# P^T by VectorE's 32x32 transposes and a trip through DRAM in a two-layer attention encoder

## The chip, the cores and the metric

The kernel runs on one core of one Trainium2 chip. The metric is the device time of one execution in microseconds, of which the median over the runs is given. Smaller is better. A core has a matrix engine (TensorE, called PE here; its weight loads are listed apart as PEld), VectorE (DVE), ScalarE (ACT), GpSimd (POOL), a queue engine (SyncE, SP) from which this kernel starts nearly all its DMA transfers, and 16 DMA engines which carry these out. TensorE takes operands from the on-chip SBUF and writes into PSUM; VectorE and ScalarE read both; DMA connects SBUF and DRAM.

## The reference

512 tokens of width 1024 pass two layers, each of them: RMS norm, one input projection (q, k, v of 16 heads of width 64, and a gate), attention, times silu(gate), an output projection, and the residual. Layer A has three groups of heads with dilated windows, merged by their softmax denominators; layer B attends to a neighbourhood on an 8 x 64 grid.

```python
def reference(x, ...):
    for i in range(DEPTH):                       # 2
        hn = rms_norm(x, norm_gain[i])
        y = mixer_a(...) if i % N_MIXERS == 0 else mixer_b(...)
        x = x + y.astype(x.dtype)

# mixer_a, of each group g (window, dilation) in ((128, 1), (512, 4), (2048, 16))
logits = jnp.einsum('brhqd,brhkd->brhqk', qb, kb) * scale + bias
p = jnp.exp(jnp.where(valid, logits, NEG_INF) - mx)
out = jnp.einsum('brhqk,brhkd->brhqd', p, vb) / denom[..., None]
# merged by softmax over the groups of log(denom) + mx; y * silu(gate) @ w_out

# mixer_b
logits = jnp.einsum('bhcqd,bhrcjd->bhcqrj', qr, kr) + bias
p = jax.nn.softmax(where(col_valid, logits, NEG_INF), axis=-1)
out = jnp.einsum('bhcqrj,bhrcjd->bhcqd', p, vr)
```

In both layers P (queries on partitions, keys along the row) has to be turned before it is multiplied with v, since TensorE sums over partitions and the keys must lie there.

## The kernel before

All is float32. A projection is made of triples (`mm3`, L211): operands are split into a high and a low part, and three matmuls of parts add up in PSUM. The weights come from DRAM in pieces of 1024 columns (`raws`, L165: `wraw`, three buffers, issued on SP), are split by ACT (`wh`, L126) and by DVE or POOL (`wl`, L130), with four buffers each, and are used by `project` and `project_t` (L230, L246) and `out_product` (L755). Heads are worked on in pairs, `hc` = 0 to 7 in each layer; "heads 0 to 13" are the pairs 0 to 6.

PE's order of work is written out by hand. `main` (L935) yields after every triple of the projections; `side` (L948) is everything else, above all the attention. `run` (L722) joins them: every matmul adds its modelled ns to `clock` (a triple of 512 columns adds 3 x 213 = 640, a triple of 384 columns 480, a 128x128 transpose 109), and whenever `clock` has reached the due time, the side work goes on to its next `yield`. `yield 2500` means: go on 2,500 modelled ns later; `yield "wait", key, 12000` means: 12,000 after the moment at which `stamp[key]` was set. So the numbers in the yields are distances in PE's order. PE executes strictly in that order. The other engines' orders, the DMA queue of SP among them, are laid down by a scheduler when the kernel is built; each engine then works through its own list and waits at semaphores.

Layer A, one pair (`attn_a`, L604): two halves `u`. In each, `scores(u)` (L610) multiplies q and k of two query tiles and two heads into four PSUM banks, `softmax` (L645) adds the bias `e0`, `e12` and takes the minimum on DVE (signs are turned round, L652, L663), the exponent on ACT (L674) and the scaling on ACT (`normalise`, L541, L542); the result is `pr`, four buffers of 128x512. Then for each of the four `pr`, `turn_p` (L678) makes four 128x128 transposes on PE into a PSUM bank and DVE copies it into `pts` (L682). After the second half `weigh` (L684) multiplies `pts` with v into one bank `o`, and `put_y` (L544) multiplies by the gate (L565) and splits the result into `y_h`, `y_l`. A pair's time in layer A is 69.9 us, in layer B 29.2 us.

Layer B (`side_b`, L830): transposes of q and k, `scores(0)`, `scores(1)` (two banks each), `turn_p` four times (four, four, three and three transposes; DVE's copy is L904), then `weigh` (L906) and `put_y`. `raw` (L396, tag `rawk`, two buffers) holds q, k, v of the pair; its v is read by `weigh`.

`bias_a` (L573) and `bias_b` (L589) load the bias tables of a pair with six DMAs on SP, from lines in DRAM which overlap from partition to partition. There are two buffers, so the loads for pair hc + 2 can start when pair hc has read its own. `residual` (L787) loads x in pieces into tiles of the tag `pt`, which is also that of `pts`.

Of the kernel before, what the change touches and what calls it, by code (L numbers as in the profile page):

```python
# [12 lines left out]
F32 = mybir.dt.float32  # L13
# [8 lines left out]
P = 128  # L22
S = 512
D = 1024
DH = 64
NHC = 8
KT = 8
# [14 lines left out]
def tile_hybrid_encoder(  # L42
# [13 lines left out]
    nc = tc.nc  # L56
# [242 lines left out]
    def tjr(t):  # L299
        return t.rearrange("p (t j r) -> p t j r", t=4, j=4)  # L300
# [93 lines left out]
    st = {}  # L394
# [194 lines left out]
    def bias_b(hc):  # L589
# [11 lines left out]
                )  # L601
        return e

    def attn_a(hc):  # L604
        e0, e12 = st.pop(("e", hc))
        q0h, q0l, q12, k0h, k0l = st.pop(("q", hc))
        k12, v12 = st.pop(("k12", hc))
        pts = {}
# [36 lines left out]
        def softmax(hd, t, lg, cs, n):  # L645
            pr = wk.tile([P, 512], F32, tag="p", name="p", bufs=4)
            mn = wk.tile([P, 4], F32, tag="mn", name="mn", bufs=4)
            if t == 0:
                nc.gpsimd.memset(pr[:, 0:64], 0.0)
            if t == 3:  # L650
                nc.gpsimd.memset(pr[:, 192:256], BIG)
            nc.vector.tensor_tensor_reduce(  # L652
                out=pr[:, cs : cs + n],
                in0=lg[:, cs : cs + n],
                in1=e0[:, hd, cs : cs + n],
                scale=1.0,
                scalar=3.0e38,
                op0=ALU.add,
                op1=ALU.min,
                accum_out=mn[:, 0:1],  # L660
            )
# [12 lines left out]
            nc.scalar.activation(row, row, AF.Exp, bias=mn[:, 1:2], scale=-1.0, accum_out=mn[:, 2:3])  # L674
            normalise(row, mn)
            return pr

        def turn_p(hd, t, pr):  # L678
            tp = bank("tp")
            for i in range(4):  # L680
                transpose(tp[:, i * P : (i + 1) * P], pr[:, i * P : (i + 1) * P])
            nc.vector.tensor_copy(pts[hd][:, t, :], tp)  # L682

        def weigh():  # L684
            o = bank("o")
            mms = []
            for g in range(2):
                for j in range(4):
                    c = 256 + P * g
                    mms.append((  # L690
                        lambda t_, j=j: tjr(t_)[:, :, j, :],
                        lambda hs, j=j, c=c: v12[:, j, c + hs.start : c + hs.stop],
                        lambda hd, c=c + 32 * j: pts[hd][:, :, c : c + 32],
                    ))
            for i in range(4):
                f, d, n = (512 * i - 384, P * i - P, P) if i else (0, 0, 384)
                mms.append((
                    lambda t_, d=d, n=n: sb(t_, d, [[n, 2], [1, P]]),
                    lambda hs, i=i: v0[hc % 2][:, i, hs],
                    lambda hd, f=f, n=384 if i else 1664: sb(pts[hd], f, [[n, 2], [1, P]]),  # L700
                ))
            side_by_side(o, mms)
            return o

        for u in range(2):
            yield 2500 if hc < NHC - 1 else 1200
            held = scores(u)
            yield 5500 if hc < NHC - 1 else 3200
            for args in held:
                turn_p(*args)  # L710
                yield 1700 if hc < NHC - 1 else None
        if hc == NHC - 1:
            yield from v_a(hc)
            stamp["ya", "turned"] = 0
        o = weigh()
        if hc == NHC - 2:
            gap[0] = cycle((500, 500, 700))
            yield "wait", ("gate", hc), 1500
        put_y(hc, o, True, hc == NHC - 1)
        yield  # L720
# [64 lines left out]
            yield from step(k, (7,))  # L785

    def residual(src):  # L787
        st["xr"] = []
        for f in range(0, KT, 2):
            if f % 4 == 0:  # L790
                xs = wk.tile([P, 4, S], F32, tag="pt", name="xr")
            nc.sync.dma_start(xs[:, f % 4 : f % 4 + 2, :], src[:, f : f + 2, :])
            st["xr"] += [xs[:, f % 4, :], xs[:, f % 4 + 1, :]]
            yield 1000

    def sink_a(f, acc):
# [19 lines left out]
    def main_b(hc):  # L816
# [10 lines left out]
        nc.scalar.activation(eg, gt, AF.Tanh, scale=0.5)  # L827
        gated(hc, gt, eg)

    def side_b(hc):  # L830
# [17 lines left out]
        put_k([(kh, kl, tp)], 3)  # L848
        stamp["qk", hc] = 0
        yield 1750  # L850
        pts = {}

        def scores(u):
            if u == 0:
                for hd in range(2):
                    pts[hd] = wk.tile([P, 4, 512], F32, tag="pt", name="pt").rearrange("p a c -> p (a c)")
            lgs = [bank("log") for _ in range(2)]
            for b in (2 * u, 2 * u + 1):
                if b < 3:
# [38 lines left out]

        def turn_p(hd, u, pr):
            tp = bank("tp")  # L900
            n = 512 if u == 0 else 384
            for i in range(n // P):
                transpose(tp[:, i * P : (i + 1) * P], pr[:, i * P : (i + 1) * P])
            nc.vector.tensor_copy(pts[hd][:, 512 * u : 512 * u + n], tp[:, :n])  # L904

        def weigh():  # L906
            o = bank("o")
            mms = []

            for d, n, m, f in (  # L910
                (64, 128, 0, 0), (0, 64, 0, 768), (192, 256, 2, 384), (448, 64, 3, 832),
                (64, 256, 1, 128), (320, 128, 3, 640),
            ):
                mms.append((
                    lambda t_, d=d, n=n: t_[:, d : d + n],
                    lambda hs, m=m: raw[:, m, 256 + hs.start : 256 + hs.stop],
                    lambda hd, f=f, n=n: pts[hd][:, f : f + n],
                ))
# [10 lines left out]
        if hc == NHC - 1:  # L929
            stamp["yb", "turned"] = 0  # L930
        o = weigh()
        put_y(hc, o, False, hc == NHC - 1)
        yield

    def main():  # L935
# [148 lines left out]
```

## Time and profile before

| | |
|---|---|
| median of 3 runs | 904.92 us (903.37 to 907.12) |
| the profiled execution, its own time | 908.62 us |
| its span, first to last instruction | 906.7 us |
| mean granted TensorE clock | 0.994 |
| DMA | 88.31 MB, mean 97 GB/s; SP's queue 29.3% of the 16 engines' span |
| tp<-ident,p: transposes of P on PE | 368 |
| L682 DVE copy pt<-tp 128x512 | 64 of 689 ns |
| L904 DVE copy pt<-tp 128x512, 128x384 | 16 of 691 ns, 16 of 558 ns |
| PE matmul o<-pt,rawk 128x128 (runs of 32), o<-pt,raw 128x128 (whole rows) | 276 ns, 285 ns |
| wraw<-in_w | 95 of 512 KB, 38 of 384 KB, 10 smaller |
| e<-l_d, eb<-lb_d, eb<-gb_d | 32 of 112 KB and 16 of 128 KB; 16 of 128 KB; 32 of 32 KB |

Matmuls overlap one another: the 272 ns that the profile gives for one transpose are its own length from start to modelled end, not its step on PE. What a piece of work costs PE is read from the chain of waits, which lists without overlap the work that ended last. The lists of DMA issues give the time at which SP handed the transfer over, not that at which it was done; how long transfers run is read from the DMA share and GB/s of short stretches. A wait is put down to the releaser that came last.

### The profile page before, as it was taken

The page shows a single profiled execution, that of the slowest core. Times are in us where ns is not written, and L with a number is a line of the kernel's source. Part 1 is how long each engine was busy: PE and PEld are TensorE (multiplying, and loading weights), DVE is VectorE, ACT ScalarE, POOL GpSimd, SP SyncE. Part 2 cuts the span into 40 slices and gives each one's busy share as a digit, 9 for nine tenths or more (in the row PEclk, how much of TensorE's full clock was granted, in tenths as well). Part 3 has the DMA queues.
Part 4 walks back from the last instruction along what each step waited for, and adds up shares of the span by engine and source line. Part 5 has one row for each costly group of instructions (what it writes and reads, how often), then busy time and mean ns, then how long its engine had stood idle before and what let it go on. Part 6 is the DMA issues. An engine that isn't in the chain of part 4 may idle for free.

```text
span 906.7 us, 15891 instructions
## 1 busy us (share of the span) xinstructions
PE 895.3 (99%) x5951; PEld 744.9 (82%) x5951; DVE 505.8 (56%) x1324; ACT 428.8 (47%) x888; POOL 301.6 (33%) x500
## 2 busy tenths in 40 slices
PE   8999999999999999999999999998999999999998
PEld 6788888888888888888888787788989988898776
DVE  7354565555555545546456656446465656565643
ACT  6435534533543553453543454443466546664551
POOL 2341441432342342332423341111434344424511
PEclk9999999999999999999999999998999999999999
DMA  6352222232223222222232221263222232222134
GB/s 235 106 154 72 87 93 88 82 92 93 74 84 111 88 80 93 90 83 94 72 102 93 70 89 38 77 208 132 94 94 77 75 105 79 86 90 91 55 122 150
DMA packets 36669, 88.31 MB, mean 97 GB/s; under 512 B 3824, under 2 KB 15024, under 8 KB 36592
## 3 DMA queue, kind: packets, MB, share of 16 engines
q1 hardware_dynamic: 36304, 87.28, 29.3%
q8 instruction: 47, 0.77, 0.4%
q14 instruction: 30, 0.25, 0.1%
q10 hardware_dynamic: 288, 0.01, 0.0%
HBM read 82.63 MB, written 4.64 MB: 96 GB/s over the span
## 4 chain that ended last, share of the span: by engine, by line
PE 94%; ACT 2%; DVE 2%; DMA 1%; issue 1%; ACTq 0%; POOLq 0%; DVEq 0%
PE acc L205 76%; PE tp L209 8%; PE log L205 5%; PE o L205 5%; ACT p L542 1%; ACT p L893 1%; DMA hg<-in_head_gain 0%; DVE hn_l L355 0%; DVE ssq L809 0%; DVE wl L130 0%; DVE xr L798 0%; ACT wh L126 0%; ACT p L674 0%; PE pk L205 0%; DVE raw L271 0%
## 5 line engine op out<-in xcount | busy, mean ns | idle before, releaser
L205 PE MATMUL acc<-wh,hn_h 128*128 128x512 f32 (+1 forms) x768 | 303.7, 395 | 3.0 <-DVE xr L798 1.1
L126 ACT CAST wh<-wraw 128x512 fp32r<-128x512 f32 (+1 forms) x276 | 161.7, 586 | 286.0 <-PE acc L205 246.4
L205 PE MATMUL acc<-wl,hn_h 128*128 128x512 f32 (+1 forms) x768 | 287.7, 375 | 0.7 <-DVE wl L130 0.7
L205 PE MATMUL acc<-wh,hn_l 128*128 128x512 f32 (+1 forms) x768 | 288.0, 375 | 0.0
L130 POOL TENSOR_TENSOR wl<-wraw,wh 128x512 fp32r<-128x512 f32 (+1 forms) x110 | 140.3, 1275 | 430.0 <-ACT wh L126 394.6
L130 DVE TENSOR_TENSOR wl<-wraw,wh 128x512 fp32r<-128x512 f32 (+1 forms) x166 | 109.8, 662 | 142.2 <-ACT wh L126 137.4
L205 PEld LDWEIGHTS acc<-wh,hn_h 128*128 128x128 f32 x768 | 145.6, 190 | 29.9 <-issue 6.2
L205 PEld LDWEIGHTS acc<-wh,hn_l 128*128 128x128 f32 x768 | 145.5, 189 | 22.1
L205 PEld LDWEIGHTS acc<-wl,hn_h 128*128 128x128 f32 x768 | 146.0, 190 | 17.7 <-DVE wl L130 1.0
L205 PE MATMUL acc<-hn_h,wh 128*128 128x512 f32 x192 | 80.1, 417 | 0.2
L205 PE MATMUL acc<-hn_h,wl 128*128 128x512 f32 x192 | 75.3, 392 | 0.0
L205 PE MATMUL acc<-hn_l,wh 128*128 128x512 f32 x192 | 75.1, 391 | 0.0
L674 ACT ACTIVATE p<-p,mn 128x512 f32<-128x512 f32 (+1 forms) x64 | 44.9, 702 | 53.0 <-DVE mn L663 53.0
L542 ACT ACTIVATE p<-p,mn 128x512 f32<-128x512 f32 (+3 forms) x128 | 69.8, 584 | 0.0
L682 DVE COPY pt<-tp 128x512 f32<-128x512 f32 x64 | 44.1, 689 | 40.1 <-PE tp L209 39.9
L257 DVE TENSOR_REDUCE ss<-sq 128x4 f32<-128x256 f32 (+1 forms) x96 | 48.4, 505 | 25.4 <-POOL sq L256 25.2
L209 PE MATMUL tp<-ident,p 128*128 128x128 f32 x368 | 55.8, 272 | 0.0
L209 PEld LDWEIGHTS tp<-ident,p 128*128 128x128 f32 x368 | 45.9, 140 | 12.0 <-ACT p L542 0.5
L205 PE MATMUL acc<-y_h,wh 128*128 128x512 f32 x128 | 51.8, 405 | 0.0
L205 PE MATMUL acc<-y_h,wl 128*128 128x512 f32 x128 | 50.0, 391 | 0.0
L205 PE MATMUL acc<-y_l,wh 128*128 128x512 f32 x128 | 50.0, 390 | 0.0
L256 POOL TENSOR_TENSOR sq<-rawq 128x512 f32<-128x512 f32 x32 | 33.3, 1058 | 45.1 <-ACT rawq L409 44.8
(136 smaller groups left out, 1155.4 us busy)
## 6 DMA issues: line engine op xcount, KB each, us to landing
wraw<-in_w SPq DMA_DIRECT2D x95, 512.0 KB
wraw<-in_w SPq DMA_DIRECT2D x38, 384.0 KB
e<-l_d SPq DMA_DIRECT2D x32, 112.0 KB
e<-l_d SPq DMA_DIRECT2D x16, 128.0 KB
eb<-lb_d SPq DMA_DIRECT2D x16, 128.0 KB
xr<-in_xg SPq DMA_DIRECT2D x4, 512.0 KB
xm_d<-xr SPq DMA_DIRECT2D x8, 256.0 KB
xr<-xm_d SPq DMA_DIRECT2D x4, 512.0 KB
```

What stands on the lines that cost most here:

```text
L126: nc.scalar.copy(h, raw)
L130: eng.tensor_sub(l, raw, h.bitcast(F32))
L205: nc.tensor.matmul(o, l, r, **kw)
L209: nc.tensor.transpose(o, i, ident)
L256: nc.gpsimd.tensor_mul(sq, raw[:, i, : ns * 64], raw[:, i, : ns * 64])
L257: nc.vector.tensor_reduce(ss[:, i * ns : (i + 1) * ns], sq.rearrange("p (a b) -> p a b", b=64), axis=AX.X, op=ALU.add)
L542: nc.scalar.activation(pr, pr, AF.Copy, scale=mn[:, 3:4])
L674: nc.scalar.activation(row, row, AF.Exp, bias=mn[:, 1:2], scale=-1.0, accum_out=mn[:, 2:3])
L682: nc.vector.tensor_copy(pts[hd][:, t, :], tp)
L893: nc.scalar.activation(pr[:, o : o + n], pr[:, o : o + n], AF.Exp, bias=mn[:, 0:1], scale=-1.0, accum_out=mn[:, 2:3])
```

## The change

For pairs 0 to 6 of both layers `turn_p` is no longer used. A new helper, `turner`, takes each `pr` through DVE's transpose, which turns every 32x32 block in its place, into a tile `tr` (one buffer, 128 partitions x 2048 elements in layer A, 1792 in layer B). What is then still missing is that blocks change places between partition groups: `tr` is written to DRAM by one DMA (`td`, two buffers), and four DMAs bring it back, each into 32 partitions of `pts`. Layer A does so once per half (two trips a pair), layer B once per pair. Pair 7 keeps the transposes on PE.

`pts` becomes one tile of 128 x 4096 with one buffer in place of two of 128 x 2048, with another order of its columns, and `weigh` reads it with other strides. `residual` takes one tile of the same size. The yields in layer A change: before, 2500, scores, 5500, four times 1700, for each half; after, 2500, scores, 8000, scores, 19000, product with v. In layer B `weigh` and `put_y` of pair hc are put into `pending` and are done in `side_b(hc + 1)`, 10000 after that pair's projection of q, k, v, ahead of its transposes of q and k, which follow 2500 later.

```diff
+    class turner:
+        def __init__(self, run):
+            self.run = run
+            self.t = wk.tile([P, 4 * run], F32, tag="tr", name="tr", bufs=1)
+
+        def put(self, src, n, off):
+            dst = sb(self.t, off, [[32, n // P], [self.run, 4], [1, 32]])
+            nc.vector.transpose(dst, src[:, :n].rearrange("p (i b k) -> p i b k", b=4, k=32))
+
+        def out(self, dst):
+            run = self.run
+            d = dr.tile([P, 4 * run], F32, tag="td", name="td", bufs=2)
+            nc.sync.dma_start(d, self.t)
+            for b in range(4):
+                nc.sync.dma_start(
+                    dst[32 * b : 32 * b + 32, :].rearrange("p (a x) -> p a x", a=4),
+                    bass.AP(d.tensor, d.offset + run * b, [[4 * run, 32], [128 * run, 4], [1, run]]),
+                )
+
     def attn_a(hc):
...
-                for hd in range(2):
-                    pts[hd] = wk.tile([P, 4, 512], F32, tag="pt", name="pt")
+                pts.append(wk.tile([P, 4096], F32, tag="pt", name="pt", bufs=1))
...
                     mms.append((
-                        lambda t_, j=j: tjr(t_)[:, :, j, :],
+                        lambda t_, j=j: sb(t_, 32 * j, [[256, 2], [P, 2], [1, 32]]),
                         lambda hs, j=j, c=c: v12[:, j, c + hs.start : c + hs.stop],
-                        lambda hd, c=c + 32 * j: pts[hd][:, :, c : c + 32],
+                        lambda hd, g=g, j=j: sb(pts[0], at(0, j, hd, 2 + g), [[2048, 2], [128, 2], [1, 32]]),
                     ))
...
-        for u in range(2):
-            yield 2500 if hc < NHC - 1 else 1200
-            held = scores(u)
-            yield 5500 if hc < NHC - 1 else 3200
-            for args in held:
-                turn_p(*args)
-                yield 1700 if hc < NHC - 1 else None
-        if hc == NHC - 1:
+        if hc < NHC - 1:
+            for u in range(2):
+                yield 2500 if u == 0 else 8000
+                turned = turner(512)
+                for hd, t, pr in scores(u):
+                    turned.put(pr, 512, 256 * hd + 128 * (t % 2))
+                turned.out(pts[0][:, 2048 * u : 2048 * u + 2048])
+            yield 19000
+        else:
+            for u in range(2):
+                yield 1200
+                held = scores(u)
+                yield 3200
+                for args in held:
+                    turn_p(*args)
+                    yield
             yield from v_a(hc)
...
     def residual(src):
-        st["xr"] = []
+        xs = wk.tile([P, KT, S], F32, tag="pt", name="xr", bufs=1)
+        st["xr"] = [xs[:, f, :] for f in range(KT)]
...
     def side_b(hc):
-        yield "wait", ("raw", hc), 12000 if hc < NHC - 1 else 11000
+        if hc:
+            yield "wait", ("raw", hc), 10000
+            pending.pop()()
+            yield 2500 if hc < NHC - 1 else 1000
+        else:
+            yield "wait", ("raw", hc), 12000
...
         for u in range(2):
             held += scores(u)
             yield 1200 if u == 0 else 2400
+        if hc < NHC - 1:
+            turned = turner(448)
+            for hd, u, pr in held:
+                turned.put(pr, 512 if u == 0 else 384, 224 * hd + 128 * u)
+            turned.out(pts[0][:, :1792])
+            pending.append(lambda: put_y(hc, weigh(), False, False))
+            return
         for args in held:
             turn_p(*args)
             yield 1000
```

More of the change, by code (lines that the diff above doesn't have):

```diff
@@ L607, in attn_a @@
         k12, v12 = st.pop(("k12", hc))
-        pts = {}
+        pts = []
+        at = lambda t, a, hd, i: 2048 * (t // 2) + 512 * a + 256 * hd + 128 * (t % 2) + 32 * i
         def scores(u):
             if u == 0:
-                for hd in range(2):
-                    pts[hd] = wk.tile([P, 4, 512], F32, tag="pt", name="pt")
+                pts.append(wk.tile([P, 4096], F32, tag="pt", name="pt", bufs=1))
             tiles = []
@@ L681, in turn_p @@
                 transpose(tp[:, i * P : (i + 1) * P], pr[:, i * P : (i + 1) * P])
-            nc.vector.tensor_copy(pts[hd][:, t, :], tp)
+            dst = sb(pts[0], at(t, 0, hd, 0), [[32, 4], [512, 4], [1, 32]])
+            nc.vector.tensor_copy(dst, tp.rearrange("p (i a r) -> p i a r", i=4, a=4))
         def weigh():
@@ L690, in weigh @@
                     mms.append((
-                        lambda t_, j=j: tjr(t_)[:, :, j, :],
+                        lambda t_, j=j: sb(t_, 32 * j, [[256, 2], [P, 2], [1, 32]]),
                         lambda hs, j=j, c=c: v12[:, j, c + hs.start : c + hs.stop],
-                        lambda hd, c=c + 32 * j: pts[hd][:, :, c : c + 32],
+                        lambda hd, g=g, j=j: sb(pts[0], at(0, j, hd, 2 + g), [[2048, 2], [128, 2], [1, 32]]),
                     ))
             for i in range(4):
-                f, d, n = (512 * i - 384, P * i - P, P) if i else (0, 0, 384)
+                (t0, i0), (t1, i1) = ((i - 1, 1), (i, 0)) if i else ((0, 0), (3, 1))
                 mms.append((
-                    lambda t_, d=d, n=n: sb(t_, d, [[n, 2], [1, P]]),
+                    lambda t_, d=P * t0, n=P * (t1 - t0): sb(t_, d, [[n, 2], [32, 4], [1, 32]]),
                     lambda hs, i=i: v0[hc % 2][:, i, hs],
-                    lambda hd, f=f, n=384 if i else 1664: sb(pts[hd], f, [[n, 2], [1, P]]),
+                    lambda hd, t0=t0, i0=i0, n=at(t1, 0, 0, i1) - at(t0, 0, 0, i0): sb(
+                        pts[0], at(t0, 0, hd, i0), [[n, 2], [512, 4], [1, 32]]
+                    ),
                 ))
@@ L787, in residual @@
     def residual(src):
-        st["xr"] = []
+        xs = wk.tile([P, KT, S], F32, tag="pt", name="xr", bufs=1)
+        st["xr"] = [xs[:, f, :] for f in range(KT)]
         for f in range(0, KT, 2):
[L790 to L793, printed above, removed]
+            nc.sync.dma_start(xs[:, f : f + 2, :], src[:, f : f + 2, :])
             yield 1000
@@ L828, in main_b @@
         gated(hc, gt, eg)
+    pending = []
     def side_b(hc):
-        yield "wait", ("raw", hc), 12000 if hc < NHC - 1 else 11000
+        if hc:
[4 more added lines that the diff above has]
+            yield "wait", ("raw", hc), 12000
         raw = st.pop(("raw", hc))
@@ L850, in side_b @@
         yield 1750
-        pts = {}
+        pts = []
+        at = lambda a, hd, i: 448 * a + 224 * hd + 32 * i
         def scores(u):
             if u == 0:
-                for hd in range(2):
-                    pts[hd] = wk.tile([P, 4, 512], F32, tag="pt", name="pt").rearrange("p a c -> p (a c)")
+                pts.append(wk.tile([P, 4096], F32, tag="pt", name="pt", bufs=1))
             lgs = [bank("log") for _ in range(2)]
@@ L900, in turn_p @@
             tp = bank("tp")
-            n = 512 if u == 0 else 384
-            for i in range(n // P):
+            n = 4 if u == 0 else 3
+            for i in range(n):
                 transpose(tp[:, i * P : (i + 1) * P], pr[:, i * P : (i + 1) * P])
-            nc.vector.tensor_copy(pts[hd][:, 512 * u : 512 * u + n], tp[:, :n])
+            dst = sb(pts[0], at(0, hd, 4 * u), [[32, n], [448, 4], [1, 32]])
+            nc.vector.tensor_copy(dst, tp[:, : n * P].rearrange("p (i a r) -> p i a r", i=n, a=4))
         def weigh():
@@ L908, in weigh @@
             mms = []
-            for d, n, m, f in (
-                (64, 128, 0, 0), (0, 64, 0, 768), (192, 256, 2, 384), (448, 64, 3, 832),
-                (64, 256, 1, 128), (320, 128, 3, 640),
-            ):
+            for d, n, m, i, a in (
+                (64, 128, 0, 0, 0), (0, 64, 0, 6, 0), (192, 256, 2, 3, 0), (448, 64, 3, 6, 2),
+                (64, 256, 1, 1, 0), (320, 128, 3, 5, 0),
+            ):
+                q = [[32, min(n // 32, 4)], [1, 32]]
+                p = [[448, min(n // 32, 4)], [1, 32]]
+                if n == 256:
+                    q, p = [[P, 2]] + q, [[32, 2]] + p
                 mms.append((
-                    lambda t_, d=d, n=n: t_[:, d : d + n],
+                    lambda t_, d=d, q=q: sb(t_, d, q),
                     lambda hs, m=m: raw[:, m, 256 + hs.start : 256 + hs.stop],
-                    lambda hd, f=f, n=n: pts[hd][:, f : f + n],
+                    lambda hd, p=p, i=i, a=a: sb(pts[0], at(a, hd, i), p),
                 ))
@@ L928, in side_b @@
             yield 1000
[L929 to L932, printed above, removed]
+        stamp["yb", "turned"] = 0
+        put_y(hc, weigh(), False, True)
         yield
```

## The prediction

> **What bounds the kernel now.** I read the page first (busy times, then the chain that ended last), then PE's waits, then the chain, ACT, the DMA queue and the DMA rates around one pass of each layer.
>
> ```profile
> PE 895.3 (99%) x5951; PEld 744.9 (82%) x5951; DVE 505.8 (56%) x1324; ACT 428.8 (47%) x888; POOL 301.6 (33%) x500
> PE 94%; ACT 2%; DVE 2%; DMA 1%; issue 1%; ACTq 0%; POOLq 0%; DVEq 0%
> ```
>
> PE is busy 99% of the span and is 94% of the chain: each instruction taken off PE shortens the run by its step, as long as PE does not wait in its place. Today its largest wait is the first line of PE's waits, and the clock after it is the second fence (columns: stretch; PE, PEld, DVE, ACT, POOL busy; granted clock; DMA share; GB/s):
>
> ```profile
> PE pk L205 <- DVE ssq L809: 1.6, 1, 1.6
> ```
>
> ```profile
> 626.00:629.00 3.00, 3.00 (x12) 3.00 (x12) 1.79 (x11) 0.09 (x1) 0.00 (x0) 0.50 0.31 114
> 629.00:632.00 3.00, 3.00 (x11) 3.00 (x10) 0.00 (x0) 0.42 (x1) 1.00 (x1) 0.50 0.00 0
> ```
>
> After 1.6 us of waiting and 1.5 us of eight one-column matmuls PE got half its clock for 6 us. With 0.91 and 0.92 granted in the 2 and 3 us beside it that is 3.4 us of full speed lost.
>
> The chain in order of time (start, us, what), head pair 4 of layer A, then one pair of layer B:
>
> ```profile
> 384.74 6.36 PE acc L205 x27
> 391.10 0.44 PE tp L209 x4
> 391.54 2.09 PE acc L205 x9
> 401.19 3.62 PE o L205 x48
> ```
>
> ```profile
> 749.70 2.83 PE acc L205 x15
> 752.52 0.44 PE tp L209 x4
> 756.47 0.33 PE tp L209 x3
> 759.92 1.69 PE o L205 x24
> ```
>
> Four transposes take 0.44 us of the chain, three 0.33 us; scores of the second half end at 384.74 and 749.70; the product with v starts 16.5 and 10.2 us later. Nine 512-column matmuls take 2.09 us, so one triple 0.697 us; a 384-column triple takes 0.527 us (1.58 us for nine). When the last P is normalised (L542) ACT's timeline shows:
>
> ```profile
> 391.58 0.72 ACT L542 ACTIVATE p<-p,mn 128x512 f32<-128x512 f32 x1
> 755.35 0.79 ACT L542 ACTIVATE p<-p,mn 128x256 f32<-128x256 f32 x2
> ```
>
> That is 7.6 us after the scores in A (392.30), 6.4 us in B (756.14). What the DMA queue of SP issues in that stretch of A, and how fast DMA moves:
>
> ```profile
> 386.81 1.10 SPq L578 DMA_DIRECT2D e<-l_d  x2
> 387.94 2.62 SPq L583 DMA_DIRECT2D e<-l_d  x4
> 392.47 60.71 SPq L174 DMA_DIRECT2D wraw<-in_w  x10
> ```
>
> ```profile
> 391.00:393.00 2.00, 2.00 (x12) 1.69 (x11) 1.29 (x3) 1.90 (x4) 0.15 (x1) 1.00 0.34 54
> 399.00:401.00 2.00, 2.00 (x10) 1.45 (x9) 1.29 (x2) 1.52 (x3) 0.39 (x1) 1.00 0.64 256
> 401.00:403.00 2.00, 2.00 (x35) 1.88 (x36) 1.00 (x2) 0.91 (x2) 2.00 (x3) 1.00 0.00 0
> ```
>
> The six bias loads for the pair after next start 2.1 us after the scores and run with about a third of the DMA engines (share 0.34 at 54 GB/s); only at 401, 16 us after the scores, are they and the weights behind them done.
>
> **What is removed.** turn_p for pairs 0 to 6. In A eight groups of four transposes a pair: 7 x 8 x 0.44 = 24.6 us. In B two groups of four and two of three: 7 x (0.88 + 0.66) = 10.8 us. Together 35.4 us of PE, all on the chain. DVE loses the copies out of PSUM (56 and 14 of 0.69 us, 14 of 0.56 us, 56 us), and gains as many 32x32 transposes of the same sizes. The trace has none. Lower end 0.4 us, the 128x256 form of other DVE rows; upper end 1.4 us, POOL's subtraction of the same tile; I take the 0.69 us of the copy, nearest in engine and size. DVE is 56% busy, so the total is free; only the last transpose of a group lies on the new path. The new strides of the product with v cost nothing: 32-element runs (o<-pt,rawk, 276 ns) and whole rows (o<-pt,raw, 285 ns) take the same today.
>
> **What is added: a trip.** P now leaves by one write of 1 MB (0.9 MB in B) and returns by four reads, all on SP: 21 x 5 = 105 issues of 0.33 to 0.6 us, some 50 us on a queue that is mostly waiting. The product with v stands in PE's fixed order, so what comes late stops PE and all matmuls behind it.
>
> Write alone: xm_d<-xr and a weight load beside it move at up to 404 GB/s (windows of 608 to 616 us), I take 390; so 1.0 us to the first bytes, 1 MB / 0.39 = 2.7 us, 0.5 us to the landing: 4.2 us, 3.9 in B. Reads alone: xr<-xm_d, four issues of 512 KB from 877.67 us, move 2 MB until about 885.7, 8.0 us, so half of it 8.0 - 2.7 = 5.3 us, 4.9 in B. These are lower ends: those rows use all 128 partitions, the reads of a block row only 32. The upper end is the rate of the bias loads, 90 GB/s at best (389 to 391 us), 12 us. I take 5.3, as rows of 1.8 and 2 KB are nearer to xr's 4 KB than to the bias loads' overlapping ones.
>
> [...]
>
> **Does the trip fit? Layer A.** The code puts the product 19,000 of its own ns after the scores, and books 640 for a triple: 30 triples, 30 x 0.697 = 20.9 us. Trip: P at 7.6, transpose 0.7, write 4.2, reads 5.3, two waits and the issues' overlap 0.2: 18.0 us. It would fit with 2.9 us to spare. But for pairs 0 to 5 the bias loads lie in its way. Today they and one weight load keep some engines until 16; the write queued behind adds its 2.7 us there, and the reads of the first half (scores now 11 us earlier, so issued about 1 us after these scores) come ahead: the write lands at 18 to 20, the reads at 23.5 to 25.5. PE waits 2.6 to 4.6 us, I take 3.5; 6 x 3.5 = 21.0 us. Pair 6 meets layer B's bias loads (384 KB instead of 704, by the issues' sizes) and fits.
>
> **Layer B.** The product of a pair is put 10,000 after the next projection of q, k, v ends: eight gate triples and eleven of 384 columns, 5.58 + 5.77 = 11.3 us. The scores of the second half now end, counted from their own projection's end, after 11.3, the product 1.7, waits of 6, 6, 4 and 3 triples (19 x 0.527 = 10.0), transposes 0.9 and scores 1.8: 25.7 us. The period is 29.2 - 1.5 = 27.7 us. So the product comes 27.7 - 25.7 + 11.3 = 13.3 us after the scores; "a projection later" is only 3 us more than today's 10.2. Trip: 6.4 + 0.6 + 3.9 + 4.9 + 0.3 = 16.1 us. SP is issuing bias loads until 756.7 (7.0 after the scores), just before the write is ready. PE waits 2.8 us, seven times: 19.6 us.
>
> **What is queued behind.** On SP the reads wait for the write, weight loads behind them: up to 9 us. That is covered: between 397.5 and 410.4 no weight load is issued today and PE does not wait. Without that cover each late load would stop PE for its delay. On DVE the scaling of y (L565) waits for the product, and splits of weights (L130) behind it; wh has four buffers of four triples each (2.8 us of PE work), so 3 us are covered.
>
> **The half clock.** Waits of 3 us are as long as the one that preceded the half clock above. Some will fall on its window and some not; I take half of 13, 6.5 x 3.4 = 22.1 us (ends 0 and 44).
>
> The sum, against the profiled execution's 908.6 us: - 35.4 + 21.0 + 19.6 + 22.1 = + 27.3, 935.9. That execution is 3.7 us above the median 904.9, so I predict **932 us**. Its own range: waits 1 us off either way (13) and the half clock at a quarter or three quarters (11): 908 to 956.
>
> **Rivals.**
>
> R1, the trip is hidden: P ready sooner, the bias loads elsewhere in the queue. 908.6 - 35.4 - 3.7 = 869.5. For it: pair 6's sum fits. Against it: seven trips of B are 2.8 us too long by lower ends. Chance 0.10.
>
> R2, one layer's trips fit, the other's do not and keep the clock: about + 20 - 35.4, 889. For it: A's own sum has 2.9 us spare. Chance 0.15.
>
> R3, all waits as forecast, and no half clock: 908.6 - 35.4 + 40.6 - 3.7 = 910 (905 to 915). For it: one case in the trace, partly tiny matmuls. [...] Chance 0.15, of it 0.07 within 0.5%.
>
> R4, reads at half the rate, whether by their 32 partitions or by two weight loads among them: 2.6 us more in A, 2.3 in B, 6 x 2.6 + 7 x 2.3 = 32; with waits of 5 to 6 us all 13 lose the clock, 44 - 22 more: 986. It decides from 190 to 220 GB/s. Chance 0.24; the port rule above is one reason for it.
>
> That the change does not do what it says: SP's order is fixed beforehand, and a write put behind a weight load that waits (up to 9.9 us today) starts late. It would look like R4.
>
> **Numbers.** Forecast 0.36, R4 0.24, R3 0.15, R2 0.15, R1 0.10. 880 to 990 leaves out R1 and the far end of R4, below 0.2. Faster by over 0.5% (what a measurement here can tell): R1 and R2, 0.25; within: 0.07; slower: 0.36 + 0.24 + 0.08 = 0.68.
>
> **What would show it.** tp<-ident,p falls from 368 to 46 on PE, and 84 DVE transposes of about 0.7 us stand in for the copies of L682 and L904. PE's waits: "PE o" on a DMA pt<-td, 3 to 4 us for pairs 0 to 5 of A and about 3 in B, with PEclk 0.5 behind some. The write lands about 18 us after the scores in A and 11 in B. I am wrong if PE's waits on pt are below 1 us, if the wait is in DVE's transposes, or if PE waits for wh and wl instead.

## The result, and the profile after

The changed kernel takes 1015.82 us (median of 4 runs, 1010.72 to 1017.41) against 905.88 us (903.37 to 907.12): a ratio of 1.1208, 95% interval 1.1160 to 1.1255, or 110 us slower. The forecast was 932 us. The sign was right, the size was not. The profiled execution has a span of 1014.0 us against 906.7 us.

The page of the changed kernel, busy times and shares of the chain that ended last (engines, then lines):

```profile
PE 891.6 (88%) x5629; PEld 739.1 (73%) x5629; DVE 505.6 (50%) x1324; ACT 423.7 (42%) x888; POOL 300.0 (30%) x500
PE 56%; DMA 18%; DVE 12%; ACT 8%; issue 3%; SPq 2%; POOL 1%; ACTq 0%; DVEq 0%; POOLq 0%
PE acc L205 42%; DMA td<-tr 10%; DMA pt<-td 7%; PE o L205 7%; PE tp L209 4%; PE log L205 3%; ACT p L542 2%; SPq L622 2%; DVE wl L130 2%; ACT p L934 2%; DVE tr L615 1%; DVE rawq L271 1%; ACT wh L126 1%; ACT rawk L409 1%; ACT p L698 1%
```

PE was 94% of the chain and is now 56%; the trip through DRAM (td<-tr out, pt<-td back) and the softmax that feeds it have taken the place. The longest waits of PE (in all, times, longest):

```profile
PE o L205 <- DMA pt<-td: 94.5, 12, 10.5
PE o L205 <- DMA wraw<-in_w: 6.6, 1, 6.6
PE o L205 <- issue: 4.5, 1, 4.5
PE acc L205 <- ACT rawk L409: 2.1, 6, 0.9
```

The first three lines are 14 waits for the same thing, P^T, one for each changed pair: 105.6 us. (The trace puts two of them down to something else, because the releaser is inferred; in pair 4 of layer A, the one called issue, the last read of P^T lands at 428.24 us and PE goes on at 428.55.) By the gaps between PE's matmuls they are 5.8, 7.6, 6.6, 5.6, 4.5, 5.8 and 3.5 us in layer A (39.3) and 6.2, 9.9, 10.2, 9.8, 10.1, 10.5 and 9.6 us in layer B (66.3). What the change set out to remove and add is there, in groups (busy, mean ns | idle before). PE's transposes of P, then VectorE's by form:

```profile
L209 PE MATMUL tp<-ident,p 128*128 128x128 f32 x46 | 7.0, 273 | 0.0
```

```profile
L615 DVE STREAM_TRANSPOSE tr<-p 128x512 f32<-128x512 f32 x70 | 47.8, 703 | 8.8 <-ACT p L542 8.3
L615 DVE STREAM_TRANSPOSE tr<-p 128x384 f32<-128x384 f32 x14 | 8.0, 574 | 0.3 <-ACT p L542 0.2
```

**Layer A, pair 4.** Second scores end at 402.90 us. The chain in order of time (start, us, what):

```profile
409.67 0.64 ACT p L542
410.32 1.33 DVE tr L615 x2
411.68 9.86 DMA td<-tr
421.56 0.32 SPq L622
421.93 0.42 SPq L622
422.40 4.76 DMA pt<-td
427.16 1.38 issue
428.55 1.51 PE o L205 x11
```

The write of 1 MB is issued 8.8 us after the scores and takes 9.86 us. It lands 18.6 us after them, and the product starts at 25.65, where PE was ready for it at 424.03 (21.1). SP's queue shows what stands ahead of it:

```profile
405.92 1.09 SPq L578 DMA_DIRECT2D e<-l_d  x2
407.06 1.09 SPq L583 DMA_DIRECT2D e<-l_d  x2
408.25 1.43 SPq L174 DMA_DIRECT2D wraw<-in_w  x1
409.73 1.75 SPq L583 DMA_DIRECT2D e<-l_d  x2
411.68 1.20 SPq L620 DMA_DIRECT2D td<-tr  x1
```

These are the six bias loads (e), as forecast, and a weight load. Around the wait, the windows (stretch; PE, PEld, DVE, ACT, POOL busy; granted clock; DMA share; GB/s):

```profile
424.00:426.00 2.00, 0.03 (x1) 0.00 (x0) 0.79 (x2) 0.74 (x2) 1.04 (x1) 1.00 0.99 210
426.00:428.00 2.00, 0.00 (x0) 0.00 (x0) 0.59 (x1) 0.00 (x0) 0.00 (x0) 0.67 1.07 240
428.00:430.00 2.00, 1.46 (x14) 1.49 (x16) 0.00 (x0) 0.00 (x0) 0.00 (x0) 0.50 0.98 399
430.00:432.00 2.00, 2.00 (x23) 2.00 (x21) 0.00 (x0) 0.00 (x0) 0.00 (x0) 0.50 0.04 10
432.00:434.00 2.00, 2.00 (x15) 1.37 (x13) 0.00 (x0) 0.00 (x0) 0.00 (x0) 0.62 0.00 0
```

The clock falls to half 2.7 us into the wait, and PE then works 5 us at half speed (428.5 to 433.5). While the reads of pt fill the DMA engines (share 0.99 and more) they move only 210 to 240 GB/s; the weights behind them, at a share of 0.98, move 399. By their semaphores the four reads of this pair land at 424.72, 425.90, 427.16 and 428.24 us; in all second halves of layer A the steps are 1.1 to 1.3 us for 256 KB, which is about 224 GB/s.

**Layer B, pair 2.** Second scores end at 779.9 us:

```profile
788.91 0.49 DVE tr L615
789.43 5.47 DMA td<-tr
794.95 0.33 SPq L622
795.33 0.42 SPq L622
795.80 0.42 SPq L622
796.27 6.37 DMA pt<-td
802.64 0.14 issue
802.77 1.30 PE o L205 x9
```

The last transpose ends 9.5 us after the scores, the write lands at 15.0, the four reads at 22.7; the product starts at 22.9, and PE was ready at 792.53, 12.6 us after the scores. A wait of 10.2 us. SP's queue between them:

```profile
788.78 0.39 SPq L174 DMA_DIRECT2D wraw<-in_w  x1
789.43 1.17 SPq L620 DMA_DIRECT2D td<-tr  x1
790.69 3.53 SPq L174 DMA_DIRECT2D wraw<-in_w  x2
794.95 1.75 SPq L622 DMA_DIRECT2D pt<-td  x4
```

Three weight loads, one ahead of the write and two between it and its reads. And the reads nearly alone on the DMA engines:

```profile
798.00:800.00 2.00, 0.00 (x0) 0.00 (x0) 0.00 (x0) 0.00 (x0) 0.00 (x0) 0.50 1.08 236
```

**The ledger of the 107.3 us** between the spans. Waits for P^T 105.6; other gaps between matmuls 6.1 (all gaps over 0.1 us: 116.4 after, 4.7 before). Work at half clock: 126.3 us of stretches, of which 55.8 are waiting, leave 70.5 us of work; at half speed that loses 35.2 us (of it 3.1 behind waits for rawq at 300 us and 1.7 behind pk, the rest behind P^T), and 5.1 are lost the same way before, so 30.1. Together + 141.8; the remainder, - 34.5, is what PE no longer does.

### The profile page after: what moved, and what is told of

It is laid out like the page before. It is cut to its first block, busy times and chain, and to the rows that moved or that the text cites. A ratio compares the mean times of both kernels' runs of the same rounds, so it can differ in the third digit from the quotient of the medians.

```text
span 1014.0 us, 15414 instructions
## 1 busy us (share of the span) xinstructions
PE 891.6 (88%) x5629; PEld 739.1 (73%) x5629; DVE 505.6 (50%) x1324; ACT 423.7 (42%) x888; POOL 300.0 (30%) x500
## 4 chain that ended last, share of the span: by engine, by line
PE 56%; DMA 18%; DVE 12%; ACT 8%; issue 3%; SPq 2%; POOL 1%; ACTq 0%; DVEq 0%; POOLq 0%
PE acc L205 42%; DMA td<-tr 10%; DMA pt<-td 7%; PE o L205 7%; PE tp L209 4%; PE log L205 3%; ACT p L542 2%; SPq L622 2%; DVE wl L130 2%; ACT p L934 2%; DVE tr L615 1%; DVE rawq L271 1%; ACT wh L126 1%; ACT rawk L409 1%; ACT p L698 1%
## 5 line engine op out<-in xcount | busy, mean ns | idle before, releaser
L205 PE MATMUL acc<-wh,hn_h 128*128 128x512 f32 (+1 forms) x768 | 301.6, 393 | 7.0 <-ACT rawk L409 2.1
L205 PE MATMUL acc<-wl,hn_h 128*128 128x512 f32 (+1 forms) x768 | 289.0, 376 | 0.4 <-DVE wl L130 0.4
L205 PE MATMUL acc<-wh,hn_l 128*128 128x512 f32 (+1 forms) x768 | 288.7, 376 | 0.0
L130 POOL TENSOR_TENSOR wl<-wraw,wh 128x512 fp32r<-128x512 f32 (+1 forms) x110 | 138.1, 1255 | 407.9 <-ACT wh L126 368.6
L130 DVE TENSOR_TENSOR wl<-wraw,wh 128x512 fp32r<-128x512 f32 (+1 forms) x166 | 114.2, 688 | 150.2 <-ACT wh L126 145.9
L205 PEld LDWEIGHTS acc<-wh,hn_h 128*128 128x128 f32 x768 | 147.0, 191 | 41.7 <-issue 8.7
L205 PEld LDWEIGHTS acc<-wh,hn_l 128*128 128x128 f32 x768 | 146.6, 191 | 21.4
L205 PEld LDWEIGHTS acc<-wl,hn_h 128*128 128x128 f32 x768 | 147.1, 192 | 18.9 <-DVE wl L130 0.9
L205 PE MATMUL o<-pt,raw 128*64 128x64 f32 (+2 forms) x192 | 24.5, 436 | 66.5 <-DMA pt<-td 66.3
L205 PE MATMUL acc<-hn_h,wh 128*128 128x512 f32 x192 | 76.5, 399 | 0.1
L565 DVE SCALAR_TENSOR_TENSOR gt<-gt,o 128x512 f32<-128x512 f32 x15 | 10.3, 688 | 132.9 <-PE o L205 132.8
L205 PE MATMUL acc<-hn_h,wl 128*128 128x512 f32 x192 | 75.1, 391 | 0.0
L205 PE MATMUL acc<-hn_l,wh 128*128 128x512 f32 x192 | 75.0, 390 | 0.0
L542 ACT ACTIVATE p<-p,mn 128x512 f32<-128x512 f32 (+3 forms) x128 | 70.8, 588 | 1.2 <-DVE mn L541 1.2
L205 PEld LDWEIGHTS o<-pt,raw 128*64 128x64 f32 x192 | 17.3, 214 | 73.5 <-issue 63.2
L205 PE MATMUL o<-pt,rawk 128*64 128x128 f32 x256 | 27.3, 399 | 39.3 <-DMA pt<-td 28.2
L615 DVE STREAM_TRANSPOSE tr<-p 128x512 f32<-128x512 f32 (+1 forms) x84 | 55.8, 682 | 9.1 <-ACT p L542 8.5
L257 DVE TENSOR_REDUCE ss<-sq 128x4 f32<-128x256 f32 (+1 forms) x96 | 47.9, 500 | 23.3 <-POOL sq L256 22.9
L205 PEld LDWEIGHTS o<-pt,rawk 128*64 128x64 f32 x256 | 24.7, 213 | 42.5 <-issue 42.5
```

What stands on the lines that cost most here:

```text
L130: eng.tensor_sub(l, raw, h.bitcast(F32))
L205: nc.tensor.matmul(o, l, r, **kw)
L257: nc.vector.tensor_reduce(ss[:, i * ns : (i + 1) * ns], sq.rearrange("p (a b) -> p a b", b=64), axis=AX.X, op=ALU.add)
L542: nc.scalar.activation(pr, pr, AF.Copy, scale=mn[:, 3:4])
L565: nc.vector.scalar_tensor_tensor(gt, gt, 0.5, o, op0=ALU.mult, op1=ALU.mult)
L615: nc.vector.transpose(dst, src[:, :n].rearrange("p (i b k) -> p i b k", b=4, k=32))
```

## The experiments

The first of TensorE's small matmuls for the sums of layer B's norm (L205, tile pk) divides the layers; the table gives when it starts, and the span behind it.

| kernel | time us | span | layer A, to pk | layer B, from pk |
|---|---|---|---|---|
| before | 905.88 | 906.7 | 625.2 | 281.5 |
| changed | 1015.82 | 1014.0 | 665.0 | 349.0 |
| e1_a_only | 950.29 | 948.5 | 666.5 | 282.0 |
| e2_b_only | 975.59 | 973.8 | 625.3 | 348.5 |
| e3_fill | 995.42 | 993.6 | 652.1 | 341.5 |
| e4_later | 884.66 | 882.4 | 615.1 | 267.3 |
| e5_nobias | 965.65 | 963.9 | 615.1 | 348.8 |
| e6_wide | 980.53 | 978.7 | 646.6 | 332.1 |
| e7_pool_queue | 1060.58 | 1058.6 | 703.0 | 355.6 |
| e8_later_14 | 866.49 | 863.1 | 597.4 | 265.7 |

All but e4 and e8 are single runs. All kernels are edits of the changed one; e8's edit is shown against e4. The kernel before ran again beside them, with medians of 903.62 us (e1 to e4) and 904.03 us (e5 to e8); the ratios of e4 and e8 are to these.

**e1 and e2: one layer alone.** e1 gives layer B back its transposes on TensorE and the product in its own pair; e2 does so for layer A.

```diff
 # e1, layer B
-        if hc:
-            yield "wait", ("raw", hc), 10000
-            pending.pop()()
-            yield 2500 if hc < NHC - 1 else 1000
-        else:
-            yield "wait", ("raw", hc), 12000
+        yield "wait", ("raw", hc), 12000 if hc < NHC - 1 else 11000
...
-        if hc < NHC - 1:
+        if False:
             turned = turner(448)
 # e2, layer A
         if hc < NHC - 1:
+            for u in range(2):
+                yield 2500
+                held = scores(u)
+                yield 5500
+                for args in held:
+                    turn_p(*args)
+                    yield 1700
+        elif False:
             for u in range(2):
                 yield 2500 if u == 0 else 8000
```

> Layer A as changed, layer B as before (P turned on PE, product with v in its own pair). Theory 'place': what costs is that PE waits for the trip at the product and then runs at half clock; the layers add up. The changed kernel reaches the row sums between the layers at 665.0 us, the kernel before at 625.2, so layer A alone should cost 40 us: 945 us, with PE waits of 3.5 to 7.6 us in seven pairs and none in B. Rival 'traffic': the trips load the DMA queue over the whole run and the loss is not bound to a layer: then the sum of this run's and the next one's loss is not the 110 us of the change.

> Layer B as changed, layer A as before. Theory 'place': the other 67 to 70 us, 974 us, with PE waits of 6 to 10.5 us at seven products of layer B and half clock after each. Rival 'traffic': B's waits grow shorter once A's trips are gone, loss well below 60 us.

Measured: 950.29 and 975.59 us, both within 6 us of what was expected. The layers hardly touch each other, so the rival of a loss by traffic over the whole run is out: layer A loses 41.3 us alone and 39.8 with B, layer B 67.0 alone and 67.5 with A. The two alone make 108.3 us together, the spans differ by 107.3. Each keeps its waits (e1: 4.0 to 7.6 us; e2: 6.4 to 10.9).

**e3: the waits filled.** Ahead of each product stand 20 (layer A) or 38 (layer B) matmuls of ones on ones whose result is not used.

```diff
         def weigh():
+            if hc < NHC - 1:
+                idle_work(20)      # 38 in layer B
             o = bank("o")
...
+    def idle_work(n):
+        busy = bank("busy")
+        for _ in range(n):
+            nc.tensor.matmul(busy, ones[:, :P], ones, start=True, stop=True)
```

> The changed kernel, with useless matmuls put on PE ahead of each product of pairs 0 to 6: 20 of 512 columns (4.6 us) in layer A, 38 (8.7 us) in layer B; nothing else differs. Theory 'place': the waits themselves stay (the useless work only fills them), the half clock goes: of some 128 us at half clock about 50 to 60 us of PE time come back, 960 us (950 to 975). Rival 'wait alone': the clock costs nothing because DMA sets the pace, 1010 to 1020 us.

The time fell by only 20 us, to 995.42, less than expected; the reason is in the filler:

```profile
L630 PE MATMUL busy<-ones 128*128 128x512 f32 x406 | 94.5, 389 | 0.0
```

94.5 us of useless work took the place of 85.4 us of gaps (31.0 are left). The half clock nearly went (13.7 us of stretches instead of 126.3), worth 35.2 - 6.8 = 28.4 us. The sum is 1014.0 - 85.4 - 28.4 + 94.5 = 994.7 for a span of 993.6. So the half clock costs about 28 us and the waits three to four times as much; my 50 to 60 us was wrong, since much of each half-clock stretch is the wait itself.

**e4: both products later.** In A the product comes 28000 (pair 6: 23000) of the code's ns after the second scores instead of 19000; in B behind the next pair's first scores instead of ahead of its q and k.

```diff
-            yield 19000
+            yield 28000 if hc < NHC - 2 else 23000
...
-        if hc:
-            yield "wait", ("raw", hc), 10000
-            pending.pop()()
-            yield 2500 if hc < NHC - 1 else 1000
-        else:
-            yield "wait", ("raw", hc), 12000
+        yield "wait", ("raw", hc), 12000 if hc < NHC - 1 else 11000
...
             yield 1200 if u == 0 else 2400
+            if u == 0:
+                if pending:
+                    pending.pop()()
+                    yield 1200
+                pts.append(wk.tile([P, 4096], F32, tag="pt", name="pt", bufs=1))
```

> The changed kernel with the product with v put later: 28000 instead of 19000 in layer A (23000 for pair 6); in layer B after the next pair's first scores, some 25 us after its own scores instead of 13, with q and k back at 12000. Theory 'place': nothing waits any more, and the 35 us of PE's transposes come back: 870 us (866 to 880), ratio 0.96, granted clock over 0.99. Rival 'traffic': the trips delay weight loads and biases, PE waits for wh and wl: 900 us or more.

884.66 us (884.12 to 890.04), ratio to before 0.9807, interval 0.9769 to 0.9845: above the 866 to 880 that were expected. No wait for P^T is left, and the same change is now 1.5 to 2.3% faster than the kernel before. Layer B gained 14.2 us, layer A only 10.1, where its transposes alone were put at 24.6. PE's first wait and ACT's timeline at one of these waits (PE idle from 232.5 to 234.3):

```profile
PE acc L205 <- ACT rawk L409: 11.0, 8, 2.4
```

```profile
231.82 0.71 ACT L542 ACTIVATE p<-p,mn 128x512 f32<-128x512 f32 x1
232.44 0.60 ACT L126 CAST wh<-wraw 128x512 fp32r<-128x512 f32 x1
232.95 0.72 ACT L542 ACTIVATE p<-p,mn 128x512 f32<-128x512 f32 x1
233.57 1.24 ACT L409 ACTIVATE rawk<-acc,rs_n 128x512 f32<-128x512 f32 x2
234.71 0.72 ACT L542 ACTIVATE p<-p,mn 128x512 f32<-128x512 f32 x1
235.32 1.24 ACT L409 ACTIVATE rawk<-acc,rs_n 128x512 f32<-128x512 f32 x2
```

The change also moved the second half's scores in layer A from 21 to 11 us behind the first's. Their softmax now meets the end of the k and v projection on ACT; PE waits for the accumulators to be emptied (L409), which stand behind exponentials and scalings (L542).

**e5: no bias loads from pair 2 on.** The tables of pairs 0 and 1 are used again for the later pairs of the layer.

```diff
     def bias_a(hc):
+        if hc > 1:
+            return kept[hc % 2]
...
+        kept[hc] = e0, e12
         return e0, e12
 # and so in bias_b
```

> The bias tables of pairs 0 and 1 of each layer are kept and used again for pairs 2 to 7, whose loads of tables are left out. Theory (the write of the turned blocks lies behind the bias loads, which go to few DMA engines): from pair 2 on layer A's second write lands about 13 us after the second scores instead of 18.6, the wait of TensorE ahead of the product falls from 5 us or so to 0 to 1 in A, and in B, where the write took 5.5 us, it falls by 1 to 2 us: A gains about 25 to 30 us, B about 6 to 10 with its half clock, 975 to 985 us. Rival (the write is slow by itself, or waits for the weight loads): the write still lands 16 us or more after the scores, the waits in A stay above 3 us, and the time stays above 1000 us.

In layer A exactly the step expected: in pair 4, whose second scores end at 367.84 us, the write is issued at 8.79 us and the reads behind it at 13.54, no longer at 18.7:

```profile
376.63 0.34 SPq L628 DMA_DIRECT2D td<-tr  x1
377.25 0.33 SPq L174 DMA_DIRECT2D wraw<-in_w  x1
381.38 1.75 SPq L630 DMA_DIRECT2D pt<-td  x4
```

A's waits are gone but for 0.45 us in pair 1 and 3.8 in pair 6, which meets layer B's first tables, and layer A ends 10.1 us earlier than before the change. That is 49.9 us back, twice what I expected: 35 are waits (39.3 to 4.3 us, in pairs 0 and 1 too, whose second writes also have no bias loads ahead of them now), and 13.7 are lost no longer by work at half clock. Layer B did not move (348.8), against an expected 6 to 10. There a weight load took the place of the bias loads: in pair 2 two weight loads now stand ahead of the write and one behind it, where it was one and two, the write takes 6.1 us for 5.5 and the reads 6.7 for 7.7. So without its bias loads B's trip is as long as with them.

How the bias loads hold the write up shows in the packet records of the changed kernel's trace: the packets of the bias loads (896 bytes) keep 4.3 of the 16 DMA engines busy on the mean at 412 to 414 and 416 to 418 us, and at 419 to 420 us, when little but the write's own packets (8 KB) is left, these are on 4.0 at a time. The share of the DMA engines is then a quarter:

```profile
420.00:422.00 2.00, 2.00 (x10) 1.67 (x9) 0.00 (x0) 0.62 (x1) 0.63 (x1) 1.00 0.24 100
```

The write took 9.86 us behind the bias loads and under 4.8 without. That its last packets are on the engines which the bias loads held is my reading; it was not shown.

**e6: reads to all partitions.** The four reads of a buffer go to 128 partitions each, with the same rows of DRAM, bytes and length of row. The blocks then do not change places between partition groups.

```diff
-                    dst[32 * b : 32 * b + 32, :].rearrange("p (a x) -> p a x", a=4),
-                    bass.AP(d.tensor, d.offset + run * b, [[4 * run, 32], [128 * run, 4], [1, run]]),
+                    dst[:, run * b : run * b + run],
+                    bass.AP(d.tensor, d.offset + run * b, [[4 * run, P], [1, run]]),
```

> Each of the four reads of a buffer goes to all 128 partitions instead of to 32 of them, with the same bytes and the same length of row; the blocks then do not change places. [...] Rival (the reads are slow because weight loads stand ahead of them in the rings, or by the length of their rows): reads still take over 7 us and the time stays within 8 us of 1016.

980.53 us, 35 us less, where the rival allowed 8. In pair 4 of layer A the first product now starts 2.7 us after the first read is issued instead of 7.0 (a quarter of the reads is enough to begin, and PE then waits in pieces, in layer A 0.3 to 2.7 us long), in pair 2 of layer B 5.9 us instead of 7.8. The DMA engines carry 296 GB/s (a window of this kernel at the reads of layer A):

```profile
410.00:412.00 2.00, 0.83 (x7) 0.35 (x5) 0.69 (x1) 1.21 (x2) 0.39 (x1) 1.00 0.99 296
```

against 210 and 240 in the changed kernel. Layer B shows it best: from the first read's issue to the last one's landing, pairs 1 to 5 take 7.5 us on the mean in the changed kernel and 5.8 here, behind the same two weight loads. In layer A, where weight loads mix with the reads, the last landing comes only 0.6 us sooner on the mean, and in pair 4 0.5 later; most of the gain there is the early start. So the reads into 32 partitions were slow by their destination: 210 to 240 GB/s in these windows of the changed kernel, and 224 by the landings. What in the chip sets this rate was not shown.

**e7: write and reads on GpSimd's queue.**

```diff
-            nc.sync.dma_start(d, self.t)
+            nc.gpsimd.dma_start(d, self.t)
...
-                nc.sync.dma_start(
+                nc.gpsimd.dma_start(
                     dst[32 * b : 32 * b + 32, :].rearrange("p (a x) -> p a x", a=4),
```

> The write and the four reads are issued from GpSimd's queue, so that SyncE goes on with weight and bias loads while a write is under way. Theory (the order of SyncE's queue costs layer B's trip some 2 us, by the two weight loads that stand between write and reads): SyncE's 79 us of waits for the write are gone, B's waits of about 10 us fall to 7 to 8, and the time falls by 12 to 20 us. Rival 1 (the loads only come earlier into the same rings, and the trip is bound by bytes): waits within 1 us of those now, 1005 to 1020 us. Rival 2 (GpSimd, which splits 110 of the weight tiles and squares q and k, stands still behind the write and then makes TensorE wait for low halves of weights): new waits of TensorE on GpSimd's tiles in every pair, 1030 us or more.

1060.58 us, 45 us worse, a time that only the second rival allowed, but not for its reason: none of PE's waits is on a tile of POOL's. GpSimd's issues and PE's waits:

```profile
L622 POOL DMA_DIRECT2D pt<-td x84 | 46.8, 563 | 95.0 <-DMA td<-tr 75.5
```

```profile
PE o L205 <- DMA pt<-td: 153.6, 14, 13.4
```

In layer A the trip itself became longer: its waits grow from 39.3 to 79.2 us, layer B's from 66.3 to 74.5. In pair 4 of layer A the write takes 11.5 us (437.32 to 448.8) and the reads 11.2 (449.08 to 460.2), where they took 9.9 and 7.0. The weight loads are not a plain reason: two run beside this write (issued at 437.04 and 440.37), but two did so in the changed kernel as well (408.25 and 412.99). Whether the sharing of the DMA engines by two queues or the issue from GpSimd makes the trip longer was not separated. The theory is refuted: B's waits, 9.8 to 12.9 us, did not fall to 7 to 8.

**e8: e4 with the second scores later.**

```diff
-                yield 2500 if u == 0 else 8000
+                yield 2500 if u == 0 else 14000
...
-            yield 28000 if hc < NHC - 2 else 23000
+            yield 24000 if hc < NHC - 2 else 20000
```

> As e4_later, with the second half's scores of layer A 14 us of planned work behind the first's instead of 8, and the product 24 us behind the second's instead of 28. Theory (the waits of 1.2 to 2.4 us per pair that e4 has left in layer A come from ScalarE, where the exponentials of the second half meet the evacuation of the k and v projection): these waits go, e4's 11.0 us on the evacuation fall below 3, and the time falls to 872 to 878 us. Rival (the second write now lands later than the product is due): new waits on the turned blocks of 1 to 4 us per pair, 885 to 905 us.

866.49 us (864.92 to 868.32), ratio to before 0.9582, interval 0.9559 to 0.9605, somewhat better than expected. The waits on ACT are gone, and the chain is PE's again:

```profile
PE 851.6 (99%) x5629; PEld 710.3 (82%) x5629; DVE 498.8 (58%) x1324; ACT 428.6 (50%) x888; POOL 295.5 (34%) x500
PE 95%; DVE 2%; ACT 1%; issue 1%; DMA 1%; ACTq 0%; DVEq 0%
```

In pairs 0 to 5 the write of A's second half still lands 18 to 19 us after its scores, behind the same bias loads; nobody waits for it, as the product is due at 26 us. The span is 43.6 us below the one before: 5.1 are the half clock at the start (1.7) and behind pk (3.4), which here did not come. About 38.5 are left for the transposes, 3 more than their 35.4; what makes up the rest was not separated. Layer B's trip shows two more things. The last transpose ends 6.2 us after the second scores, not 9.5, as these now come 6.1 us behind the first and not 2.7. And one weight load stands between write and reads, not two; from first issue to last landing the reads of pairs 1 to 5 then last 6.1 to 7.6 us, 6.7 on the mean, where they lasted 7.2 to 7.9, 7.5 on the mean.

## Why the prediction failed, by its own steps

The forecast was 27.3 us more than before, and the spans differ by 107.3. Of the 80.0 us between them, the waits of layer B are 46.7, those of layer A 18.3, the half clock 8.0, other gaps of PE, for which the sum had no term, 6.1, and the transposes 0.9.

- **Transposes of TensorE, - 35.4.** Right: - 34.5 as the remainder of the changed kernel's ledger, 35.6 as that of e3's (906.7 + 26.3 of gaps + 1.7 of half clock + 94.5 of filler - 993.6), at most about 38.5 in e8.
- **VectorE's transposes, 0.69 us.** Right: 703 ns, and 574 for the smaller form.
- **The bias loads in the way of A's write, landing at 18 to 20 us.** Right in place and size (18.6; e5 takes it away).
- **A's waits, 6 x 3.5 = 21.0.** Mis-sized, 39.3. In pair 4 the reads take 7.0 us to the product, not 5.3: I took the row of the residual's reads, which go to 128 partitions, while these go to 32, and e6 shows that this counts (for layer B's reads 7.5 us into 32, 5.8 into 128). In pairs 0 to 3 and 5 the write also lands later (19.8 to 20.6 us). And pair 6, which I let fit, did not: its last transpose ends 11.0 us after the scores, and its write, issued 3.4 us behind layer B's first bias loads, takes 6.3 us for the 4.2; e5, which keeps those loads, keeps the wait (3.8 us).
- **B's trip, 16.1 us against 13.3, waits of 2.8. This is the step that failed.** The trip is 22.9 us and the waits 9.5 on average, 66.3 in all for 19.6. The product was due 12.6 us after the scores, near the 13.3. The excess of 6.8 us in pair 2 is: 2.5 because the last transpose ends 9.5 and not 7.0 us after the scores; 1.6 because the write takes 5.5 and not 3.9 us, with a weight load of 384 KB ahead of it; 2.6 because the reads take 7.8 and not 5.2 us. On the mean of pairs 1 to 5 the reads take 7.5 us; e6 puts 1.7 of that down to the narrow destination, and e8, with one weight load ahead of them in place of two, takes 0.8 less (e5, also with one, 0.7 less). Together they are about the excess. That the second weight load is the cause rests on this comparison of kernels, which differ in more than that. For the late transposes the trace has this reason: the 6.4 us for P were taken from the kernel before, where the softmax ran ahead of the next projection's end. The move put the scores beside that end, and ACT empties four accumulators into raw (779.1 to 783.2) among the exponentials, while DVE does sums of squares and splits among the minima. e8, with the halves further apart, is back at 6.2; an experiment with that alone was not made, so this part is argued.
- **The half clock, 22.1.** Near in its sum, 30.1 more than before by the trace and 28.4 by e3, but by luck: every one of the 14 waits had a stretch of it, not half of 13, and each lost about 2.2 us of work, not 3.4, since part of a stretch is the wait itself. The window on which some waits fall and some not was an estimate that the one case of the trace before did not show; the runs show steps of 3.413 us and how much idleness within one brings half clock (last section).
- **The queue behind.** The cover held: PE waits 0.4 us in all for wl and 0.3 for wh in the changed kernel, though SP spends 79 us waiting for the writes.
- **The rivals.** R3 fell with the clock (over 1.9 us of idleness within one step was always enough, last section), R2 with both layers' waits. R4 (986 us, half the rate of the reads) was nearest, and both its reasons were at work, the destination of 32 partitions (1.7 us by e6) and the two weight loads (0.8 us by e8); that a rule of the chip stands behind the first, on which its chance leans, no run shows. R4's waits of about 6 us were near layer A's 5.6 on the mean, but its 5 us in layer B were too short for the 9.5, as it knew nothing of the late transposes and the longer write. R1 was not the kernel's case but names what the change can give: 869.5 us was its price, and e8 takes 866.5.

## What to carry to other kernels

A trip through DRAM for which no engine waited cost nothing that showed here (e8), and one that ended 3.5 to 10.5 us after its consumer was due cost three times the work that it saved (105.6 us of waits for some 35). Sum a trip with the transfers that share its DMA engines at that moment, in the order of the queue, not with a rate from a quiet stretch. Where a consumer stands in a fixed order, move it back until the trip fits (in e8 by 5 us in layer A and 10 in layer B), and look at what the move lays on top of each other on the other engines. Before a change is given up for its waits, try it with the consumer later: with the same number of instructions on each engine it took 1016 us and 866 us.

## What the runs showed of the hardware

- Half clock came in whole steps of 3.4 us (3.4, 6.8, 10.2, 13.7), and within a trace its stretches begin whole multiples of 3.413 us apart: in the changed kernel at 119.49, 198.00 and 273.09 us, which are 23 and 22 steps.
- What counted is how long PE is idle within one such step. Over the ten traces (first 5 us left out), a step at full clock with under 1.5 us of idleness was never followed by half clock (2493 steps), one with over 1.9 us always was (77), and of the 28 between 9 were. So the place of a wait against the steps decided, beside its length. A wait of about 1.65 us ahead of the same small matmuls (pk) was followed by 6.8 us of half clock before the change and 3.4 in e4, where it lay in one step, and by none in e8, where the edge of two steps cuts it in half. In e4 two waits of 1.2 and 0.9 us in one step had 3.4 us of half clock behind them, and a wait of 1.8 us across an edge (to 234.3 us) had none.
- A wait broken by work did not save the clock: in e6 layer A's waits come in pieces of 0.3 to 2.7 us between matmuls, and five of its seven pairs of the change still fall to half clock.
